# Five of six half gates as fixed-order groups with seven-product pairs, block sums one piece later, and an adding DMA for part of FF2's sums

## The chip, the cores and the metric

The kernel runs on one core of one Trainium2 chip. The metric is the device time of one execution in microseconds (us). Before the change three runs took 1454.71, 1454.83 and 1456.06 us, with a median of 1454.83.

## The reference

The kernel computes one layer of a decoder trunk on 256 tokens of width D = 2048, in float32. The three token mixers (attention, gated linear attention, gated MLP) give y_a, y_b and y_c; they lie ahead of the change. What follows is

```
merged = sigmoid(ga)*(y_a @ wa) + sigmoid(gb)*(y_b @ wb) + sigmoid(gc)*(y_c @ wc)
h   = x + merged @ w_o
out = h + square(relu(rms_norm(h, g2) @ w1)) @ w2      # D_FF = 8192
```

Here ga, gb and gc (2048 columns each) are columns of rms_norm(x, g1) @ w_in; y_a and y_c are 512 wide, y_b is 1024 wide.

## The kernel before, in words

**Float32 by three products.** TensorE multiplies in fp32r. Each operand is split in a high part (a copy to fp32r by ScalarE, "hi") and a rest (a subtraction by VectorE, "lo"), and each product of a 128x128 activation block and a 128x512 weight block is three matmuls: hi*hi, hi*lo, lo*hi. Weights stream from HBM in 1 MB loads and are split on the way, so every weight costs ScalarE and VectorE one pass each.

**Groups of fixed order.** From w_o on, the work is a list of groups. A group makes 256 x 1024 outputs from 2048 rows of weights: eight pairs `kp` of 128-row weight blocks, taken in the order `ORDER`. A pair is a 2x2 by 2x2 block product (two token halves, two row blocks, two column halves). `P` pairs do it with eight block products (24 matmuls, one piece). `S` pairs do it with seven (Winograd's form of Strassen's algorithm: 21 matmuls) in two pieces, `A` (9 matmuls) and `B` (12). An `S` pair needs sums of weight blocks (tile `fsum`, lines 807 to 809) and sums of activation blocks (lines 683 to 689; tiles `hS`, `fS`, `mS`), and four more accumulators, `P1`, `P5`, `P6`, `P7`, beside `c11` to `c22`: all eight PSUM banks. `seven` folds them into a tile `fu` at the group's last piece. w_o has two groups; then come four phases (`ph`), each of two groups of FF1 and two of FF2 (n = 0, 1).

**Order of work.** Inside `manual_schedule` TensorE, ScalarE, VectorE and SyncE run in the order in which the code issues. At piece i the loop issues `ready(i + 2)` (load, weight sums, split), then the matmuls of piece i; there are three buffers for split weights (`fhi`, `flo`) and three for raw ones (`fraw`), so the split of piece i+2 waits until TensorE has finished piece i-1. What a group leaves (turning its result into the next operand by eight TensorE transposes per half, line 664, splitting it, and its block sums) is issued during the first pieces of the next group. The norm of h before FF1 needs only 1/rms per token: its square is multiplied in when FF2's result is added to h (line 914).

**The gates before.** The six half gates (three gates, two column halves; the code takes them in four 512-column steps) and the branch products run in `group_a`, with two-row-block pieces of 12 matmuls, no seven-product pairs, and a sigmoid and a multiplication per 512 columns (lines 691 to 726).

Line 768 is every matmul of the groups, 794 and 795 the split, 221 to 223 the matmuls of `group_a`, 203 and 204 its split.

Of the kernel before, what the change touches and what calls it, by code (L numbers as in the profile page):

```python
# [63 lines left out]
def trunk(ctx: ExitStack, tc: tile.TileContext, x, rpe_table, norm1_g, w_in, q_norm_g, k_norm_g,  # L64
# [626 lines left out]
    mg, mS = None, {}
    for n in range(D // 512):
        gts = []
        for i in range(3):
            pg = group_a(w_in[0], 0, KT, C_GATE + i * D + n * 512, 512, xT)
            if mg is None:
                drain()
                br_ctx.__exit__(None, None, None)
                early_ctx.__exit__(None, None, None)
                mpool = ctx.enter_context(tc.tile_pool(name="mpool", bufs=1))  # L700
                mg_ctx = tc.tile_pool(name="mg", bufs=1)
                mg = mg_ctx.__enter__()
                mT = mpool.tile([P, KT, 2 * T], F32R, tag="act2", name="mT")
            if i == 0 and n == D // 512 - 1:
                gt = [mpool.tile([P, 512], F32, tag="half", name="half", bufs=2) for tt in range(NT)]
            else:
                gt = mg.tile([P, NT, 512], F32, tag=f"gt{i}", name=f"gt{i}", bufs=1 + (i == 0))
                gt = [gt[:, tt, :] for tt in range(NT)]
            for tt in range(NT):
                nc.scalar.activation(gt[tt], pg[tt], AF.Sigmoid, scale=r[:, tt:tt + 1])  # L710
            gts.append(gt)
        for i, (wsrc, k0, nk) in enumerate(((w_br_a, 0, 4), (w_br_b, 4, 8), (w_br_c, 12, 4))):
            pp = group_a(wsrc[0], 0, nk, n * 512, 512, yT, k0=k0)
            for tt in range(NT):
                nc.vector.tensor_mul(gts[i][tt], pp[tt], gts[i][tt])
                if i:
# [283 lines left out]
```

## Time and profile before

| what | number |
|---|---|
| median of three runs | 1454.83 us |
| the profiled execution: own time, span | 1454.36 us, 1452.6 us |
| TensorE, VectorE, ScalarE busy | 1422.9, 1072.9, 766.5 us |
| gates and branches, 296.90 to 649.00 | 352.10 us |
| w_o, 649.00 to 742.68 | 93.68 us |
| first phase of FF, 742.68 to 925.09 | 182.41 us |
| second phase, 925.09 to 1098.92 | 173.83 us |

The stages are cut at the first matmul of each. Phases three and four repeat the second. Matmuls overlap in the trace (one is shown for about 390 ns and the next starts 227 ns later), so waits of TensorE are read from the starts, not from its busy share.

### The profile page before, as it was taken

What the parts mean: (1) busy time and instruction counts of PE and PEld (TensorE: products, weight loads), DVE (VectorE), ACT (ScalarE), POOL (GpSimd) and SP (SyncE); (2) the same over time, 40 slices, a digit from 0 to 9 for tenths busy, and PEclk for the clock granted to TensorE, in tenths of its full rate; (3) what the DMA queues carried; (4) which work ended last, traced back from release to release, by engine and by line L of the source; (5) the groups of instructions that cost most, each with busy time, mean ns of one, the idle gap of its engine ahead of it and who ended that gap; (6) DMA issues with size and microseconds to landing.
All of it is one profiled execution on the core that took longest, in us unless ns stands there. A gap on an engine that the chain in (4) does not pass through costs nothing.

```text
span 1452.6 us, 16287 instructions
## 1 busy us (share of the span) xinstructions
PE 1422.9 (98%) x6452; PEld 1168.5 (80%) x6452; DVE 1072.9 (74%) x1160; ACT 766.5 (53%) x827; POOL 14.0 (1%) x37
## 2 busy tenths in 40 slices
PE   8999999999999999999998999999999999999998
PEld 6899887788888888877886878888788887888776
DVE  5655655454645546457898989999999999999898
ACT  7457444454444444445656654466644665546653
POOL 2000000000000000000000000000000000000000
PEclk9999999999999999999999999999999999999999
DMA  8555554545555555545555555666456555555553
GB/s 290 183 181 165 182 176 133 184 151 199 192 185 203 177 199 187 190 158 193 199 185 192 173 175 197 208 203 203 147 200 207 199 203 174 201 190 194 198 195 124
DMA packets 101948, 272.20 MB, mean 187 GB/s; under 512 B 4748, under 2 KB 11440, under 8 KB 101872
## 3 DMA queue, kind: packets, MB, share of 16 engines
q1 hardware_dynamic: 100944, 268.59, 55.0%
q0 software_dynamic: 928, 2.57, 0.5%
q8 instruction: 50, 0.82, 0.2%
q14 instruction: 26, 0.21, 0.0%
HBM read 268.26 MB, written 2.88 MB: 187 GB/s over the span
## 4 chain that ended last, share of the span: by engine, by line
PE 70%; DVE 18%; issue 6%; ACT 5%; DMA 0%; SPq 0%; DVEq 0%; ACTq 0%
PE c L768 22%; PE ga L221 14%; PE ga L223 14%; PE ga L222 14%; DVE flo L795 8%; PE P L768 4%; DVE fsum L807 3%; ACT fhi L794 3%; DVE fsum L808 2%; DVE fsum L809 2%; PE tt L235 1%; DVE fT L175 1%; PE pst L590 0%; ACT sums L688 0%; ACT half L675 0%
## 5 line engine op out<-in xcount | busy, mean ns | idle before, releaser
L204 DVE TENSOR_TENSOR wlo<-wraw,whi 128x1024 fp32r<-128x1024 f32 (+3 forms) x232 | 266.2, 1152 | 248.6 <-ACT whi L203 248.4
L203 ACT ACTIVATE whi<-wraw 128x1024 fp32r<-128x1024 f32 (+3 forms) x232 | 231.4, 1002 | 292.4 <-PE ga L223 284.9
L794 ACT ACTIVATE fhi<-fraw 128x2048 fp32r<-128x2048 f32 (+2 forms) x145 | 252.9, 1750 | 163.6 <-PE c L768 115.3
L795 DVE TENSOR_TENSOR flo<-fraw,fhi 128x2048 fp32r<-128x2048 f32 (+2 forms) x145 | 300.0, 2080 | 48.0 <-ACT fhi L794 48.0
L221 PE MATMUL ga<-whi,xT 128*128 128x512 f32 (+2 forms) x768 | 297.8, 388 | 0.0
L222 PE MATMUL ga<-wlo,xT 128*128 128x512 f32 (+2 forms) x768 | 293.4, 382 | 0.0
L223 PE MATMUL ga<-whi,xT 128*128 128x512 f32 (+2 forms) x768 | 293.1, 382 | 0.0
L768 PE MATMUL c<-fhi,hT 128*128 128x512 f32 x736 | 237.7, 390 | 0.0
L768 PE MATMUL c<-fhi,fT 128*128 128x512 f32 x736 | 237.1, 390 | 0.0
L221 PEld LDWEIGHTS ga<-whi,xT 128*128 128x128 f32 x768 | 144.6, 188 | 29.8 <-issue 3.9
L223 PEld LDWEIGHTS ga<-whi,xT 128*128 128x128 f32 x768 | 144.6, 188 | 26.9
L222 PEld LDWEIGHTS ga<-wlo,xT 128*128 128x128 f32 x768 | 144.7, 188 | 25.0
L768 PEld LDWEIGHTS c<-fhi,hT 128*128 128x128 f32 x736 | 138.2, 188 | 28.6
L768 PEld LDWEIGHTS c<-fhi,fT 128*128 128x128 f32 x736 | 138.2, 188 | 28.4
L794 ACT ACTIVATE fhi<-fsum 128x1024 fp32r<-128x1024 f32 x104 | 108.6, 1059 | 85.7 <-DVE fsum L807 41.0
L768 PE MATMUL c<-flo,fT 128*128 128x512 f32 x368 | 143.7, 391 | 3.3 <-DVE flo L795 3.3
L768 PE MATMUL c<-flo,hT 128*128 128x512 f32 x368 | 143.2, 389 | 0.0
L795 DVE TENSOR_TENSOR flo<-fsum,fhi 128x1024 fp32r<-128x1024 f32 x104 | 122.5, 1219 | 1.4 <-ACT fhi L794 1.4
L768 PE MATMUL P<-fhi,sums 128*128 128x512 f32 x312 | 106.0, 394 | 4.2 <-ACT fhi L794 4.0
L768 PEld LDWEIGHTS c<-flo,fT 128*128 128x128 f32 x368 | 69.1, 188 | 19.1 <-DVE flo L795 4.9
L768 PEld LDWEIGHTS c<-flo,hT 128*128 128x128 f32 x368 | 69.1, 188 | 14.1
L768 PEld LDWEIGHTS P<-fhi,sums 128*128 128x128 f32 x312 | 59.3, 190 | 18.4 <-ACT fhi L794 6.3
(260 smaller groups left out, 1427.1 us busy)
## 6 DMA issues: line engine op xcount, KB each, us to landing
fraw<-in_w_ff_dram SPq DMA_DIRECT2D x128, 1024.0 KB, 5.0
wraw<-in_w_in_dram SPq DMA_DIRECT2D x80, 1024.0 KB, 4.9
fraw<-in_w_o_dram SPq DMA_DIRECT2D x16, 1024.0 KB, 5.3
wraw<-in_w_br_b_dram SPq DMA_DIRECT2D x8, 1024.0 KB, 5.0
wraw<-in_w_in_dram SPq DMA_DIRECT2D x8, 692.0 KB, 4.1
wraw<-in_w_br_a_dram SPq DMA_DIRECT2D x4, 1024.0 KB, 4.9
wraw<-in_w_br_c_dram SPq DMA_DIRECT2D x4, 1024.0 KB, 5.4
wraw<-in_w_in_dram SPq DMA_DIRECT2D x6, 512.0 KB, 11.4
```

Source lines behind the costliest of these rows:

```text
L175: nc.vector.tensor_tensor(lo, ps, hi.bitcast(F32), ALU.subtract)
L203: nc.scalar.activation(hi[:, j:j + per, :w], src, AF.Copy)
L204: nc.vector.tensor_tensor(lo[:, j:j + per, :w], src, hi[:, j:j + per, :w].bitcast(F32), ALU.subtract)
L221: mm(ps[tt][:, :w], xh, hi[:, j, :w], start=(k == 0), stop=False)
L222: mm(ps[tt][:, :w], xh, lo[:, j, :w], start=False, stop=False)
L223: mm(ps[tt][:, :w], xl, hi[:, j, :w], start=False, stop=(k == nk - 1))
L768: mm(self.banks[role], a, w, start=(n == 0), stop=(n == self.total[role] - 1))
L794: nc.scalar.activation(hi[:, i:e], src[:, i - a:e - a], AF.Copy)
L795: nc.vector.tensor_tensor(lo[:, i:e], src[:, i - a:e - a], hi[:, i:e].bitcast(F32), ALU.subtract)
L807: nc.vector.tensor_tensor(ts[:, 0:2], raw[:, 1:3], raw[:, 0:1].to_broadcast([P, 2, GW]), ALU.add)
L808: nc.vector.tensor_add(ts[:, 2], ts[:, 0], raw[:, 2])
L809: nc.vector.tensor_add(ts[:, 3], ts[:, 2], raw[:, 3])
```

## The change

- Half gate (a, columns 0 to 1023) stays in `group_a` form. While its second 512 columns run, the block sums of x for pairs 2, 3, 5 and 6 are made from fresh transposes of h, which still holds x (`xs_turn`: 16 transposes).
- The other five half gates become groups with `ORDER_G`: pairs 2, 3, 5, 6 with seven products, the rest with eight. The branch products become groups of 2, 4 and 2 `P` pieces; half 0 runs first, then half 1. The merged result is turned into yT's memory.
- w_o keeps two seven-product pairs, now 2 and 3, in the order P0 P1 P6 P7 S2 P4 S3 P5. FF1 and FF2 keep three.
- `weight_sums` for an `A` piece is issued one piece earlier. `block_sums` are issued one piece after the turn, and their split one piece after that. The squares for the norm move one piece later.
- 1/rms is multiplied in at FF1's relu (line 906 of the new kernel); r2 gets its square root and one refining step. In phases 0 to 2 FF2 adds only its four `c` banks to h by VectorE; the tile `fu` is added to h by one accumulating DMA of 1 MB from GpSimd's queue (line 938). `fu` has three buffers; hS takes two of them for the whole FF part.

```diff
-ORDER_O = "P0 P1 P2 P3 P4 S6 S7 P5".split()
+ORDER_O = "P0 P1 P6 P7 S2 P4 S3 P5".split()
+ORDER_G = "P0 P1 S2 S3 P4 S5 S6 P7".split()
...
+    def block_sums(a, s):
+        b = a.rearrange("p j (t c) -> p (j t) c", c=P)
+        nc.vector.tensor_sub(b[:, 3], b[:, 1], b[:, 3])
...
+        def split():
+            nc.scalar.activation(s[:, 0], b, AF.Copy)
+            nc.vector.tensor_tensor(s[:, 1], b, s[:, 0].bitcast(F32), ALU.subtract)
+        return split
...
+    def weight_sums(q, raws):
+        raw = raws[q]
+        ts = ffp.tile([P, 4, GW], F32, tag="fsum", name="fsum")
...
             def relu(c):
                 for tt in range(NT):
-                    nc.scalar.activation(u[:, 2 * tt + c], u[:, 2 * tt + c], AF.Relu)
-            relu(1)
+                    nc.scalar.activation(u[:, 2 * tt + c], u[:, 2 * tt + c], AF.Relu,
+                                         scale=r2[:, tt:tt + 1])
...
-            nc.vector.scalar_tensor_tensor(hv, src, r2[:, tt:tt + 1], hv, op0=ALU.mult, op1=ALU.add)
+            nc.vector.tensor_add(hv, src, hv)
...
         def first(g):
-            u = seven(g)
-            for tt, c in ((0, 1), (1, 1), (0, 0), (1, 0)):
-                into(tt, c, u[:, 2 * tt + c])
+            g.u = u = seven(g)
+            if ends:
+                for tt, c in ((0, 1), (1, 1), (0, 0), (1, 0)):
+                    into(tt, c, u[:, 2 * tt + c])
...
+            if not ends:
+                nc.gpsimd.dma_start(h[:, :, n * W2:(n + 1) * W2], g.u.rearrange("p (t c) w -> p t (c w)", t=NT),
+                                    accum_op=ALU.add)
...
+    def branch_in(i, hf):
+        def last(g):
+            u = gates[i, hf]
+            for tt in range(NT):
+                for c in (1, 0):
+                    v = u[:, 2 * tt + c]
+                    nc.vector.tensor_mul(v, g.banks[f"c{tt + 1}{2 - c}"], v)
+            if i:
+                m = gates[0, hf]
+                nc.vector.tensor_add(m, m, u)
...
+    for hf in range(2):
+        for i, (wsrc, k0, nk) in enumerate(((w_br_a, 0, 4), (w_br_b, 4, 8), (w_br_c, 12, 4))):
+            if (i, hf) != (0, 0):
+                groups.append(Group(w_in[0], 0, C_GATE + i * D + hf * W2, xT, xS, ORDER_G, *gate_in(i, hf)))
+            groups.append(Group(wsrc[0], 0, hf * W2, yT, {}, [f"P{j}" for j in range(nk // 2)], *branch_in(i, hf), k0))
...
+            if i + 1 < len(pieces) and pieces[i + 1][1] == "A":
+                weight_sums(pieces[i + 1][3], raws)
```

**VectorE, first pieces of FF2's first group**, from the weight sums of its first seven-product pair (fsum) on. In the names `flo` is a weight rest, `fT` FF2's activations, `half` the tile in which block sums are made, `sums` and `kinds` where their rest goes. Before:

```order
L807 TENSOR_TENSOR fsum<-fraw 128x1024
L808 TENSOR_TENSOR fsum<-fsum,fraw 128x512
L809 TENSOR_TENSOR fsum<-fsum,fraw 128x512
L795 TENSOR_TENSOR flo<-fraw,fhi 128x1536
L175 TENSOR_TENSOR fT<-half,fT 128x2x256 x2
L683 TENSOR_TENSOR half<-half 128x128
L684 TENSOR_TENSOR half<-half 128x128
L685 TENSOR_TENSOR half<-half 128x128
L686 TENSOR_TENSOR half<-half 128x128
L689 TENSOR_TENSOR sums<-half,sums 128x512
L795 TENSOR_TENSOR flo<-fsum,fhi 128x1024 x2
L795 TENSOR_TENSOR flo<-fraw,fhi 128x2048
```

After:

```order
L781 TENSOR_TENSOR flo<-fraw,fhi 128x1536
L688 TENSOR_TENSOR half<-half 128x128
L689 TENSOR_TENSOR half<-half 128x128
L690 TENSOR_TENSOR half<-half 128x128
L691 TENSOR_TENSOR half<-half 128x128
L180 TENSOR_TENSOR fT<-half,fT 128x2x256 x2
L781 TENSOR_TENSOR flo<-fsum,fhi 128x1024 x2
L688 TENSOR_TENSOR half<-half 128x128
L689 TENSOR_TENSOR half<-half 128x128
L690 TENSOR_TENSOR half<-half 128x128
L691 TENSOR_TENSOR half<-half 128x128
L695 TENSOR_TENSOR kinds<-half,kinds 128x512
```

The weight sums now stand ahead of these rows, the second half of fT ahead of the second block sums, and the rest of the block sums (`kinds`) no longer right behind the sums but a piece later; ScalarE's copies for it move in the same way.

**VectorE, end of an FF2 group**, from `seven` on. Before:

```order
L840 TENSOR_TENSOR fu<-fu,P_6310 128x512
L841 TENSOR_TENSOR fu<-fu,P_6306 128x512
L842 TENSOR_TENSOR fu<-P_6302,fu 128x512
L843 TENSOR_TENSOR fu<-P_6302,fu 128x512
L914 SCALAR_TENSOR_TENSOR h<-fu,r_4800,h 128x512 x4
L795 TENSOR_TENSOR flo<-fraw,fhi 128x2048
L914 SCALAR_TENSOR_TENSOR h<-c_6136,r_4800,h 128x512
L914 SCALAR_TENSOR_TENSOR h<-c_6140,r_4800,h 128x512
L914 SCALAR_TENSOR_TENSOR h<-c_6150,r_4800,h 128x512
L914 SCALAR_TENSOR_TENSOR h<-c_6154,r_4800,h 128x512
L795 TENSOR_TENSOR flo<-fraw,fhi 128x2048
```

After:

```order
L832 TENSOR_TENSOR fu<-fu,P_6335 128x512
L833 TENSOR_TENSOR fu<-fu,P_6331 128x512
L834 TENSOR_TENSOR fu<-P_6327,fu 128x512
L835 TENSOR_TENSOR fu<-P_6327,fu 128x512
L781 TENSOR_TENSOR flo<-fraw,fhi 128x2048
L921 TENSOR_TENSOR h<-c_6165,h 128x512
L921 TENSOR_TENSOR h<-c_6169,h 128x512
L921 TENSOR_TENSOR h<-c_6179,h 128x512
L921 TENSOR_TENSOR h<-c_6183,h 128x512
L781 TENSOR_TENSOR flo<-fraw,fhi 128x2048
```

The four additions of `fu` to h are gone (a DMA of GpSimd's queue does them), and the four of the banks are plain additions.

**VectorE, end of the last branch group, ahead of w_o.** `wlo`, `gt` and `half` are the old form's weight rest and gates, `yT` the merged operand, `c` the branch product, `fu` gates and merged sum. Before:

```order
L715 TENSOR_TENSOR gt_4496<-ga_4679,gt_4496 128x512
L717 TENSOR_TENSOR half<-half,gt_4496 128x512 x2
L715 TENSOR_TENSOR gt_4637<-ga_4752,gt_4637 128x512
L717 TENSOR_TENSOR half<-half,gt_4637 128x512
L715 TENSOR_TENSOR gt_4637<-ga_4753,gt_4637 128x512
L717 TENSOR_TENSOR half<-half,gt_4637 128x512
L795 TENSOR_TENSOR flo<-fraw,fhi 128x1024 x2
L795 TENSOR_TENSOR flo<-fraw,fhi 128x2048 x3
```

After:

```order
L688 TENSOR_TENSOR half<-half 128x128
L689 TENSOR_TENSOR half<-half 128x128
L690 TENSOR_TENSOR half<-half 128x128
L691 TENSOR_TENSOR half<-half 128x128
L977 TENSOR_TENSOR fu<-c_4742,fu 128x512
L977 TENSOR_TENSOR fu<-c_4738,fu 128x512
L977 TENSOR_TENSOR fu<-c_4756,fu 128x512
L977 TENSOR_TENSOR fu<-c_4752,fu 128x512
L980 TENSOR_TENSOR fu<-fu 128x2048
L781 TENSOR_TENSOR flo<-fraw,fhi 128x2048
```

Where multiplications and additions of 512 columns stood, block sums (the second four of eight), four multiplications and a 2048-column addition now stand; w_o's second turn needs that addition.

## Rows read from the trace of the kernel before

**Rows 1.** Page, part 1: engine, busy us (share of span) xinstructions.
```profile
PE 1422.9 (98%) x6452; PEld 1168.5 (80%) x6452; DVE 1072.9 (74%) x1160; ACT 766.5 (53%) x827; POOL 14.0 (1%) x37
```

**Rows 2.** Chain that ended last: start us, us, engine, tile, line, instructions.
```profile
1178.47 11.56 PE c L768 x51
```

**Rows 3.** Windows: stretch us, busy PE PEld DVE ACT POOL, clock, DMA share, GB/s.
```profile
296.90:649.00 352.10, 352.10 (x1571) 291.51 (x1569) 185.57 (x183) 157.79 (x164) 0.00 (x0) 1.00 0.57 188
...
649.00:742.68 93.68, 89.83 (x398) 73.12 (x396) 77.02 (x80) 50.48 (x53) 0.00 (x0) 0.98 0.58 197
...
742.68:925.09 182.41, 175.42 (x781) 142.90 (x780) 165.26 (x173) 107.09 (x109) 0.00 (x0) 0.99 0.55 184
...
925.09:1098.92 173.83, 171.57 (x765) 140.23 (x764) 158.94 (x156) 97.98 (x87) 0.00 (x0) 1.00 0.57 194
...
1010.60:1057.04 46.44, 44.45 (x200) 35.77 (x199) 42.01 (x47) 28.36 (x29) 0.00 (x0) 1.00 0.52 181
...
1057.04:1098.92 41.88, 41.77 (x184) 34.27 (x183) 38.42 (x36) 20.82 (x15) 0.00 (x0) 1.00 0.60 204
...
1140.81:1184.43 43.62, 43.57 (x200) 35.93 (x199) 40.07 (x41) 27.97 (x28) 0.00 (x0) 1.00 0.56 190
...
652.10:655.40 3.30, 3.30 (x9) 2.52 (x9) 2.99 (x2) 0.00 (x0) 0.00 (x0) 0.50 0.94 344
```

**Rows 4.** Timeline, TensorE: start us, us, line, tiles [idle before <- releaser].
```profile
651.81 0.61 PE L768 MATMUL c<-flo,mT 128*128 128x512 f32 x1 [2.42 <-DVE flo L795]
...
762.63 0.39 PE L768 MATMUL c<-fhi,hT 128*128 128x512 f32 x1
...
767.02 0.50 PE L768 MATMUL P<-fhi,sums 128*128 128x512 f32 x1 [4.00 <-ACT fhi L794]
...
1030.95 0.50 PE L768 MATMUL P<-fhi,sums 128*128 128x512 f32 x1
...
1032.21 0.50 PE L768 MATMUL P<-flo,sums 128*128 128x512 f32 x1 [0.76 <-DVE flo L795]
```

**Rows 5.** Timeline, TensorE, eight transposes and the matmul behind them.
```profile
664.22 1.03 PE L235 MATMUL tt<-ident,half 128*128 128x128 f32 x8
...
665.01 0.48 PE L768 MATMUL c<-fhi,mT 128*128 128x512 f32 x1
```

**Rows 6.** Timeline, ScalarE, in the group from 1010.60.
```profile
1029.31 0.63 ACT L688 ACTIVATE sums<-half 128x512 fp32r<-128x512 f32 x1 [3.85 <-DVE half L686]
```

**Rows 7.** Timeline, VectorE, in the same group.
```profile
1033.68 2.29 DVE L795 TENSOR_TENSOR flo<-fraw,fhi 128x2048 fp32r<-128x2048 f32 x1 [0.39 <-ACT fhi L794]
...
1045.13 1.75 DVE L795 TENSOR_TENSOR flo<-fraw,fhi 128x1536 fp32r<-128x1536 f32 x1
```

**Rows 8.** Groups by line and shape: xcount | busy us, mean ns | idle before.
```profile
L795 DVE TENSOR_TENSOR flo<-fraw,fhi 128x2048 fp32r<-128x2048 f32 x91 | 206.7, 2287 | 48.0 <-ACT fhi L794 48.0
...
L795 DVE TENSOR_TENSOR flo<-fsum,fhi 128x1024 fp32r<-128x1024 f32 x104 | 122.5, 1219 | 1.4 <-ACT fhi L794 1.4
...
L795 DVE TENSOR_TENSOR flo<-fraw,fhi 128x1536 fp32r<-128x1536 f32 x52 | 91.1, 1751 | 0.0
...
L807 DVE TENSOR_TENSOR fsum<-fraw 128x1024 f32<-128x1024 f32 x52 | 63.5, 1222 | 0.6
...
L685 DVE TENSOR_TENSOR half<-half 128x128 f32<-128x128 f32 x17 | 5.0, 293 | 0.6
...
L841 DVE TENSOR_TENSOR fu<-fu,P 128x512 f32<-128x512 f32 x18 | 12.4, 687 | 0.6
...
L914 DVE SCALAR_TENSOR_TENSOR h<-fu,r,h 128x512 f32<-128x512 f32 x32 | 21.9, 747 | 0.0
```

**Rows 9.** DMA issues: count, KB each, median us from issue to landing.
```profile
fraw<-in_w_ff_dram SPq DMA_DIRECT2D x128, 1024.0 KB, 5.0
...
bdram<-brow POOLq DMA_DIRECT2D x2, 384.0 KB, 2.6
...
bias<-bdram POOLq DMA_DIRECT2D x1, 512.0 KB, 7.2
```

More of the change, by code (lines that the diff above doesn't have):

```diff
@@ L691, in trunk @@
[L691 to L716, printed above, removed]
-                    nc.vector.tensor_add(gts[0][tt], gts[0][tt], gts[i][tt])
-        later()
-        ks = [n * 4, n * 4 + 2]
-        srcs = [[gts[0][tt][:, (2 * jp + j) * P:(2 * jp + j + 1) * P] for j in range(2) for tt in range(NT)]
-                for jp in range(2)]
-        if n < D // 512 - 1:
-            for k, s in zip(ks, srcs):
-                later(lambda k=k, s=s: turn_into(mT, [k], [s]))
-        else:
-            later(lambda: turn_into(mT, ks, srcs, None, mS))
@@ L739, in trunk, with __init__ @@
-    r2 = gpool.tile([P, NT], F32, name="r2")
-    hs = gpool.tile([P, NT], F32, name="hs")
+                rest.append(lambda a=a, s=kinds[k // 2]: block_sums(a, s))
+        return both(rest)
     W2 = 2 * GW
     class Group:
-        def __init__(self, src, r0, c0, act, sums, order, first, last):
+        def __init__(self, src, r0, c0, act, sums, order, first, last, k0=0):
             self.src, self.r0, self.c0, self.act, self.sums, self.order = src, r0, c0, act, sums, order
+            self.k0 = k0
@@ L933, in trunk @@
+    for n in range(2):
+        groups.append(Group(w_o[0], 0, n * W2, mT, mS, ORDER_O, *residual(n)))
     for ph in range(FF // D):
[L934 removed]
         for n in range(2):
[L936 removed]
+            groups.append(Group(w_ff1[0], 0, ph * D + n * W2, "hT", hS, ORDER, *square_in(ph, n)))
         for n in range(2):
[L938 removed]
+            groups.append(Group(w_ff2[0], ph * D, n * W2, "fT", fS, ORDER, *add_in(ph, n)))
@@ L965, in trunk @@
             ready(i + LEAD)
-            since = i - done
-            if since == 1 and after:
-                after[0]()
-            multiply(piece, wts.pop(i), half=after[2] if since == 2 and after else None)
-            if since == 1 and after:
-                after[1]()
-            if since == 2 and len(after) > 3:
-                after[3]()
-            step()
+            run(i, "early")
+            multiply(piece, wts.pop(i), half=lambda: run(i, "half"))
+            run(i, "half")
+            run(i, "late")
             if ends:
-                after, done = g.last(g), i
+                for (d, when), fn in zip(((1, "early"), (1, "late"), (2, "half"), (3, "early")), g.last(g)):
+                    todo.setdefault((i + d, when), []).append(fn)
 _INS = ['x', 'rpe_table', 'norm1_g', 'w_in', 'q_norm_g', 'k_norm_g', 'gla_lr_w', 'gla_lr_b', 'gla_out_g',
```

186 lines of the change are left out of this document (133 added, 53 removed).

## The prediction

> **What bounds the kernel now.** I read the page first: TensorE is busy 98% of the span, VectorE 74%, ScalarE 53% [rows 1]. A busy TensorE may still be waiting, so the next thing is its pace. In the chain that ended last, 51 matmuls of 128x512 take 11.56 us where nothing stops them, 0.2267 us each [rows 2]. Eight transposes take 0.79 us from the first to the next matmul, 0.099 each [rows 5]. With these two prices each stage of the windows [rows 3] is checked: what is left is time in which TensorE stood still.
>
> Gates and branches: 1536 matmuls are 348.2 us, the other 35 instructions about 3.5, together 351.7 of 352.10. No waits. VectorE is busy only 185.57 us there. A phase of FF: 4 groups of 5 x 24 + 3 x 21 = 183 matmuls are 165.9 us, 32 transposes 3.2, together 169.1 of 173.83: 4.7 us of waits. By groups: a group without turns needs 41.5 us and with 16 transposes 43.1. The first FF2 group takes 46.44 (3.4 lost), the second 41.88 (0.4), FF1's first the same, FF1's second 43.62 (0.55). The first phase takes 182.41, 8.6 more than the second; 1.6 of that are 16 transposes for hT, 7.0 are waits in FF1's first group. w_o: 372 matmuls (84.3), 24 transposes (2.4), so 7.0 of 93.68 are lost.
>
> The timeline shows who is waited for. In FF2's first group the seven-product piece B of pair 3 gets its split late: TensorE starts at 1030.95 and next at 1032.21, waiting for VectorE's `flo` [rows 4], and ScalarE had stood 3.85 us at its copy of block sums which VectorE was still making [rows 6]. Everything queued behind that copy, the splits included, came late. In FF1's very first group it is the same, with four squares behind it: TensorE stands from 762.63 to 767.02 for ScalarE's `fhi`. w_o begins with 2.42 us for VectorE [rows 4]; in the stretch from 652.10 the granted clock is 0.50, the 1.2 GHz level, with 9 matmuls in 3.30 us, which costs 3.30 - 9 x 0.2267 = 1.3 us [rows 3].
>
> The 0.4 us of the quiet groups come from another place. Pairs 5 and 6 follow each other. A seven-product pair asks of VectorE 1.22 + 2 x 0.69 for the sums, 1.75 and 2 x 1.22 for the splits, 6.8 us [rows 8], against 21 x 0.2267 = 4.76 us of TensorE. VectorE can't start this earlier, since P4's split waits for a buffer of TensorE (0.39 idle), and 11.45 us pass from that split to the split of A6 [rows 7].
>
> **The change, part by part.** *Matmuls.* Each half gate with four seven-product pairs has 4 x 24 + 4 x 21 = 180 matmuls for 192. Five of them save 60 x 0.2267 = 13.6 us. The 16 transposes for x's block sums cost 1.6. All of it lies on TensorE's stream: **-12.0**.
>
> *VectorE in the gates.* A half gate now asks 4 x 6.8 + 4 x 2.29 + 8 x 0.69 = 41.8 us of VectorE [rows 8] against 180 x 0.2267 = 40.8 of TensorE. The branch groups behind it give some back: for b (four pieces, four multiplications, one 2048-column addition at a split's 2.29) 14.2 against 21.8, for c 9.6 against 10.9, for a 7.3 against 10.9. Over the five gates and six branches VectorE has 271, with two turns 278, of 291 us. So the cover is thin, but it holds on the whole; S5 and S6 stand where they stand in FF, so each gate should lose what a quiet FF group loses, 0.39. Five times that is **+2.0**. Both ends: 0 (VectorE has run ahead), and 2 us for each of the five gates' last two pairs, with nothing saved up, 5 x 2 x (6.8 - 4.76) = 20.
>
> *Into w_o.* From the end of the last gate VectorE's queue holds a split 2.29, four additions 2.75, a split 2.29, two rests 1.37, a split 2.29, eight block sums of 0.29, four multiplications 2.75 and the addition 2.29: 18.4 us [rows 8]. TensorE asks for that sum after two branch pieces, eight transposes and one w_o piece, 10.9 + 0.8 + 5.4 = 17.1. That is 1.3 us of waiting if VectorE never stands, and up to 5 with a stand like that of rows 6. I take 4, plus 1.3 for a fallen clock and 0.7 for the rest, 6 in place of 7: **-1.0**, between -4 and +2.
>
> *FF1's first group.* The block sums' copies leave ScalarE's way and the squares come one piece later. VectorE's queue up to P4: splits 2.29, 2.29, 1.75 and 2.44, four additions 2.75, weight sums 2.6, four rests 2.75, eight block sums 2.3, one more rest 0.69, 19.9 us, against 16.3 + 1.6 of TensorE up to A3's start; the split of P4 waits for ScalarE's squares. From there 11.45 to A6's split, with another rest 0.69 and about 1 us (an estimate: seven tiny instructions) for the root. A6's split would end near 35, TensorE asks at 33. With about 1 us at P4 and A5 I get 3.0 for 7.0: **-4.0**, between -6.5 and 0.
>
> *FF2's first group, four times.* The same sum, without squares and root: P4's split can begin at 19.9, A6's at 19.9 + 11.45 + 0.69 = 32.0, and it ends at 33.7; TensorE asks at 33.1. So 0.6, taken as 1.0, for 3.4. The other three groups keep theirs: order and buffers round P4, S5, S6 are as before, and weight sums issued a piece earlier stand at the same place of VectorE's queue there. 4 x 2.4: **-10**, between -14 and 0.
>
> *The adding DMA.* It takes four additions of 0.747 us from VectorE in six groups, and four more get 0.06 shorter [rows 8], 19 us of VectorE in all. They stood at the end of a group, ahead of P pieces, where VectorE has slack. I cost it at **nothing**; if that slack is gone, a part of the -10 hangs on it. New waits: the DMA waits for the four bank additions, and nothing else is queued on GpSimd. The next `seven` waits for the DMA, since hS holds two of the three `fu` buffers: ScalarE's first copy of `seven`, with the splits of the next group queued behind it, and TensorE behind those. From issue to that copy there are 41.5 - 5.4 - 4.7 = 31 us (a group, less its last piece, less the split and additions ahead of the issue). The nearest rows: 1 MB of weights lands in 5.0 us; GpSimd's queue took 2.6 for 384 KB and 7.2 for 512 KB [rows 9]. At the slowest of these, and twice over because h is read too, 1 MB takes 28.8. It fits. I take 10.
>
> The Trainium skill, page SBUF - State Buffer, section Who interferes with whom, says that VectorE with two SBUF inputs excludes a GpSimd instruction that reads SBUF, and that a DMA "stalled" by VectorE is one whose descriptors GpSimd could not write. No run here shows an adding DMA beside such work; it would lengthen the 10 us and is in the third rival below.
>
> Sum: -12.0 + 2.0 - 1.0 - 4.0 - 10 = -25. The profiled execution took 1454.36 us (a span of 1452.6 and 1.8 round it), 0.5 below the median of the runs. 1454.4 - 25 = **1429**.
>
> **Rivals.** *VectorE becomes the bound of the gates.* For it: 41.8 against 40.8, and only two pieces of lead. Against it: quiet FF groups ask 31.8 + 5.5 = 37.3 of VectorE and lose only 0.4 with the same sequence at their end. It costs 12 to 20 us in place of 2: about 1443. Chance 0.17.
>
> *FF keeps its waits.* For it: VectorE's queue in FF2's first group is as long as before but for 3 us. Against it: ScalarE's stand of 3.85 us, which the new order removes. It takes back up to 14: about 1441. Chance 0.13.
>
> *VectorE is what limits FF everywhere.* For it: 158.94 of 173.83 us, 91% [rows 3]; then its 19 us less come off whole, 9 more than my 10: about 1420. Against it: the 0.39 idle of rows 7. Chance 0.08. The Trainium skill, Perfetto Trace Analysis, section Identifying the Most-Contended Engine, says just this: judge TensorE by its weight loads (here 140.23 of 173.83, 81%) and VectorE by occupancy, so VectorE comes first. The waits counted from starts, 4.7 of 173.83, don't agree with it.
>
> *The adding DMA holds up `seven`: slower.* Six times X - 31 us, X being the time from issue to landing. From X = 35 on it eats the 25 us; at X = 40 the kernel takes about 1483. For it: an adding DMA is in no row. Against it: 28.8 as the slow bound. Chance 0.05.
>
> **Numbers.** My forecast has 0.55, the rivals 0.17, 0.13, 0.08 and 0.05; 0.02 is left for no change. The range from 1419 to 1445 takes in both ends of the middle cases and leaves out the DMA's and the worst gates. A measurement of this kernel tells 0.2%, 2.9 us, from no change. Faster: 0.92, all but the last two. Same: 0.03. Slower: 0.05.
>
> **What would show it.** Gates and branches (to w_o's first matmul) 11 us shorter, with waits of about 0.4 us at the second seven-product pair before each gate's end and nowhere else; ScalarE no longer standing for `half` in FF2's first group, and that group at 44 us; the other groups still 41.9 and 43.6; FF1's first group 4 us shorter; one wait of some 4 us after w_o's first piece; no wait on the software DMA queue. I am wrong if a gate group takes over 43 us, if FF2's first group stays above 46, or if `seven` waits for the DMA.

## The result, and the profile after

The changed kernel takes 1432.64 us (median of four runs, 1430.41 to 1432.99), the kernel before 1454.77 beside it: a ratio of 0.984, with a 95% interval from 0.983 to 0.986. The forecast was 1429, in a range from 1419 to 1445. The profiled execution took 1432.36 us, 22.0 less than that of before.

The page after, engines, queue and issues of the adding DMA (the last number is us from issue to landing), against [rows 1, 9]:

```profile
PE 1408.1 (98%) x6408; PEld 1158.8 (81%) x6408; DVE 1155.1 (81%) x1232; ACT 795.2 (56%) x826; POOL 21.2 (1%) x43
...
q0 software_dynamic: 2560, 8.86, 3.3%
...
h<-fu POOLq DMA_DIRECT2D x6, 1024.0 KB, 9.4
```

The windows after, by stage and then by group, in the columns of [rows 3]: gates and branches, w_o, the first and the second phase, w_o's first group, FF1's first group, FF2's two groups of phase 2.

```profile
297.90:643.52 345.62, 342.61 (x1517) 281.57 (x1516) 290.25 (x272) 185.84 (x156) 0.00 (x0) 1.00 0.58 198
643.52:733.77 90.25, 88.15 (x406) 73.05 (x404) 76.73 (x82) 51.36 (x57) 0.00 (x0) 1.00 0.54 181
733.77:909.56 175.79, 173.13 (x782) 141.89 (x781) 161.33 (x172) 107.72 (x111) 1.24 (x1) 1.00 0.60 198
909.56:1081.19 171.63, 170.72 (x766) 140.39 (x764) 152.30 (x148) 97.77 (x87) 2.40 (x2) 1.00 0.65 209
643.52:689.80 46.28, 44.18 (x204) 36.49 (x203) 38.79 (x43) 24.29 (x23) 0.00 (x0) 1.00 0.51 169
733.77:779.82 46.05, 44.21 (x201) 35.77 (x200) 44.64 (x56) 30.77 (x39) 0.00 (x0) 1.00 0.54 182
995.05:1039.31 44.26, 43.60 (x201) 35.92 (x199) 41.41 (x46) 28.21 (x29) 0.00 (x0) 1.00 0.57 191
1039.31:1081.19 41.88, 41.77 (x185) 34.27 (x183) 35.57 (x32) 20.82 (x15) 1.19 (x1) 1.00 0.73 229
```

Stage by stage against [rows 3]: gates and branches 352.10 to 345.62 (-6.5), w_o 93.68 to 90.25 (-3.4), the first phase 182.41 to 175.79 (-6.6), each later phase 173.83 to 171.6 (-2.2). Ahead of the gates the time is 1.0 us longer (the stretch begins at 297.90, not at 296.90). A gate group takes 41.20 us (42.11 where eight transposes lie in it); VectorE's work in gates and branches has grown from 185.57 to 290.25.

Two timelines tell what is new. ScalarE after, where the second 512 columns of the first half gate begin:

```profile
312.67 1.06 ACT L208 ACTIVATE whi<-wraw 128x1024 fp32r<-128x1024 f32 x1 [1.47 <-issue]
319.42 0.69 ACT L1046 ACTIVATE fu<-ga,r 128x512 f32<-128x512 f32 x1 [5.69 <-PE ga L228]
320.78 0.69 ACT L1046 ACTIVATE fu<-ga,r 128x512 f32<-128x512 f32 x1 [0.67 <-PE ga L228]
321.37 2.94 ACT L208 ACTIVATE whi<-wraw 128x1024 fp32r<-128x1024 f32 x3
```

TensorE after: at the same place, into w_o, and in FF2's first group:

```profile
320.36 0.39 PE L228 MATMUL ga<-whi,xT 128*128 128x512 f32 x1
322.47 0.51 PE L226 MATMUL ga<-whi,xT 128*128 128x512 f32 x1 [1.72 <-ACT whi L208]
323.73 0.80 PE L227 MATMUL ga<-wlo,xT 128*128 128x512 f32 x1 [0.75 <-DVE wlo L209]
...
648.74 0.39 PE L754 MATMUL c<-fhi,yT 128*128 128x512 f32 x1
651.22 0.98 PE L240 MATMUL tt<-ident,fu 128*128 128x128 f32 x7 [2.10 <-DVE fu L980]
...
1028.12 0.39 PE L754 MATMUL P<-fhi,fT 128*128 128x512 f32 x1
1029.16 0.50 PE L754 MATMUL P<-flo,fT 128*128 128x512 f32 x1 [0.66 <-DVE flo L781]
```

The sigmoid of the first 512 columns is issued ahead of the weight splits of the next 512, and it needs the end of the matmuls. ScalarE stands 5.69 us, then splits three weights in a row, and TensorE waits twice, 1.88 + 1.03 us from start to start (less one pitch). No step of the forecast had this place.

### The profile page after: what moved, and what is told of

Read it like the earlier page. It is cut to its first block, busy times and chain, and to the rows that moved or that the text cites. A ratio compares the mean times of both kernels' runs of the same rounds, so it can differ in the third digit from the quotient of the medians.

```text
span 1430.7 us, 16240 instructions
## 1 busy us (share of the span) xinstructions
PE 1408.1 (98%) x6408; PEld 1158.8 (81%) x6408; DVE 1155.1 (81%) x1232; ACT 795.2 (56%) x826; POOL 21.2 (1%) x43
## 4 chain that ended last, share of the span: by engine, by line
PE 72%; DVE 18%; issue 5%; ACT 4%; DMA 0%; SPq 0%; DVEq 0%; ACTq 0%
PE c L754 41%; DVE flo L781 9%; PE ga L226 7%; PE ga L227 7%; PE ga L228 7%; PE P L754 6%; DVE fsum L787 4%; ACT fhi L780 3%; DVE fsum L788 2%; DVE fsum L789 2%; PE tt L240 1%; PE pst L595 0%; PE po L619 0%; DMA h<-in_x_dram 0%; PE po L614 0%
## 5 line engine op out<-in xcount | busy, mean ns | idle before, releaser
L780 ACT ACTIVATE fhi<-fraw 128x2048 fp32r<-128x2048 f32 (+2 forms) x201 | 352.9, 1757 | 292.0 <-PE c L754 231.4
L781 DVE TENSOR_TENSOR flo<-fraw,fhi 128x2048 fp32r<-128x2048 f32 (+2 forms) x201 | 416.7, 2083 | 92.8 <-ACT fhi L780 90.7
L209 DVE TENSOR_TENSOR wlo<-wraw,whi 128x1024 fp32r<-128x1024 f32 (+3 forms) x120 | 128.7, 1082 | 101.6 <-ACT whi L208 101.4
L208 ACT ACTIVATE whi<-wraw 128x1024 fp32r<-128x1024 f32 (+3 forms) x120 | 112.4, 946 | 120.4 <-PE ga L228 113.3
L226 PE MATMUL ga<-whi,xT 128*128 128x512 f32 (+2 forms) x448 | 174.2, 390 | 1.7 <-ACT whi L208 1.7
L227 PE MATMUL ga<-wlo,xT 128*128 128x512 f32 (+2 forms) x448 | 170.1, 380 | 0.8 <-DVE wlo L209 0.8
L228 PE MATMUL ga<-whi,xT 128*128 128x512 f32 (+2 forms) x448 | 169.6, 379 | 0.0
L754 PE MATMUL c<-fhi,yT 128*128 128x512 f32 x464 | 146.4, 390 | 0.0
L754 PE MATMUL P<-fhi,kinds 128*128 128x512 f32 x432 | 144.7, 389 | 0.0
L754 PE MATMUL c<-fhi,xT 128*128 128x512 f32 x400 | 130.7, 389 | 0.0
L226 PEld LDWEIGHTS ga<-whi,xT 128*128 128x128 f32 x448 | 85.1, 190 | 19.7 <-issue 3.9
L228 PEld LDWEIGHTS ga<-whi,xT 128*128 128x128 f32 x448 | 85.1, 190 | 14.6
```

The lines of the kernel that those rows point to most:

```text
L208: nc.scalar.activation(hi[:, j:j + per, :w], src, AF.Copy)
L209: nc.vector.tensor_tensor(lo[:, j:j + per, :w], src, hi[:, j:j + per, :w].bitcast(F32), ALU.subtract)
L226: mm(ps[tt][:, :w], xh, hi[:, j, :w], start=(k == 0), stop=False)
L227: mm(ps[tt][:, :w], xh, lo[:, j, :w], start=False, stop=False)
L228: mm(ps[tt][:, :w], xl, hi[:, j, :w], start=False, stop=(k == nk - 1))
L754: mm(self.banks[role], a, w, start=(n == 0), stop=(n == self.total[role] - 1))
```

## The experiments

Every kernel but the last two is the changed kernel with the edit shown; each was timed beside the kernel before. Single executions of the changed kernel lie 2.6 us apart, but a group's length repeats to 0.05 us where TensorE's clock does not fall, so small effects are read from group lengths. Below, "w_o", "FF1" and "FF2" are w_o's first group (46.3 us), FF1's first group of phase 1 (46.1) and FF2's first groups (44.2).

| kernel | median us | ratio to before (95%) | w_o | FF1 | FF2 |
|---|---|---|---|---|---|
| changed | 1432.64 | 0.984 (0.983 to 0.986) | 46.3 | 46.1 | 44.2 |
| sums in the turn | 1444.48 | 0.993 (0.992 to 0.994) | 51.3 | 51.1 | 45.0 |
| VectorE adds | 1430.84 | 0.983 (0.982 to 0.985) | 46.3 | 46.1 | 44.2 |
| weight sums late | 1431.37 | 0.984 (0.983 to 0.985) | 47.9 | 45.3 | 44.2 |
| relu early | 1433.31 | 0.985 (0.984 to 0.986) | 47.9 | 46.1 | 44.2 |
| sums and relu | 1451.62 | 0.998 (0.997 to 0.999) | 50.9 | 52.3 | 46.6 |
| all order undone | 1449.25 | 0.996 (0.995 to 0.997) | 51.2 | 50.1 | 46.4 |
| split with the sums | 1454.20 | 0.999 (0.999 to 1.000) | 50.9 | 52.3 | 45.6 |
| sigmoid behind | 1427.86 | 0.981 (0.980 to 0.983) | 46.3 | 46.1 | 44.2 |
| one seven-product pair | 1439.75 | 0.989 (0.988 to 0.991) | 46.3 | 46.1 | 44.3 |
| three moves | 1423.29 | 0.978 (0.977 to 0.980) | 44.1 | 44.3 | 44.3 |
| pairs apart | 1422.25 | 0.977 (0.976 to 0.979) | 44.1 | 44.2 | 44.2 |
| four pairs in FF | 1498.74 | 1.030 (1.029 to 1.031) | 46.9 | 53.6 | 51.2 |

**Block sums back in the turn.**

```diff
-                rest.append(lambda a=a, s=kinds[k // 2]: block_sums(a, s))
+                if dst is not None:
+                    block_sums(a, kinds[k // 2])()
+                else:
+                    rest.append(lambda a=a, s=kinds[k // 2]: block_sums(a, s))
```

> The changed kernel (1432.6 us), but the block sums of a turn and their copy and rest are issued inside the turn again (hT, fT, mT; x's stay deferred). Theory: ScalarE's copy of block sums, waiting for VectorE at the head of ScalarE's queue, was what cost FF2's first groups and FF1's first group their time, so both come back: FF2's first groups from 44.2 to about 46.4 us, four times 2.2, and the first phase's FF1 first group about 3 us longer; together +10 to +13, 1443 to 1446 us. Rival (the shorter VectorE queue, through the adding DMA and the additions taken from it, is what shortened these groups): they stay near 44.2 to 45, and the time within 1432 to 1436 us.

+11.8 us, the size expected, but the place is not: w_o lost 5.1, FF1 5.0, FF2's first groups only 0.8 each and not 2.2. So the deferral is worth most where the forecast had least, and something else carries 1.4 of the 2.2 in FF2.

**No adding DMA.**

```diff
-            if ends:
-                for tt, c in ((0, 1), (1, 1), (0, 0), (1, 0)):
-                    into(tt, c, u[:, 2 * tt + c])
+            for tt, c in ((0, 1), (1, 1), (0, 0), (1, 0)):
+                into(tt, c, u[:, 2 * tt + c])
...
-            if not ends:
-                nc.gpsimd.dma_start(h[:, :, n * W2:(n + 1) * W2], g.u.rearrange("p (t c) w -> p t (c w)", t=NT),
-                                    accum_op=ALU.add)
```

> The changed kernel (1432.6 us), but no adding DMA: in all FF2 groups VectorE adds the four sums to h at the group's end, as before. Theory: VectorE has slack at that place, and the DMA was worth nothing: 0 to +1.5 us, 1432 to 1434 us, with FF2's first groups at 44.2 and the FF1 groups behind an FF2 group at 41.9. Rival (VectorE limits FF everywhere, so its additions count whole): six times 4 x 0.747 and four times 0.06 a group, about +18 us, 1450 us. Middle (a part of the 2.2 us in FF2's first groups hung on VectorE's slack): +2 to +9.

Nothing, as expected: 1.8 us less in the median, inside the spread. FF2's second group in this kernel's windows, with four additions more on VectorE (37.94 us for 35.57) and the length unchanged:

```profile
1039.54:1081.42 41.88, 41.77 (x185) 34.27 (x183) 37.94 (x36) 20.84 (x15) 0.00 (x0) 1.00 0.60 204
```

**Weight sums late.**

```diff
-            if i + 1 < len(pieces) and pieces[i + 1][1] == "A":
-                weight_sums(pieces[i + 1][3], raws)
...
-            split2(hi, lo, 0, 3, raw[0][:, 1:4])
+            weight_sums(q, raws)
+            split2(hi, lo, 0, 3, raw[:, 1:4])
```

> The changed kernel (1432.6 us), but the sums of a seven-product pair's weights are made when its piece A is prepared, as before, and not behind the piece that goes ahead of it. Theory: the order on VectorE's queue barely changes, so 0 to +1.5 us, 1432 to 1434. Rival (the sums a step earlier are what lets the splits of the seven-product pieces come in time): TensorE waits again ahead of the pieces of type B, some 1 us in each of 13 groups with turns, 1440 to 1446 us.

Nothing in FF (44.2; FF1 even 0.8 shorter). The 1.6 us in w_o is TensorE's clock, which fell behind the same wait of 2.26 us, told at the end.

**Relu early, and what goes with it.** Three kernels: relu alone; with the block sums; with the weight sums too.

```diff
+            relu(1)
...
-            return [lambda: (relu(1), relu(0)) and None, lambda: turns(made["fT"], n, 1, src, None, fS, AF.Square),
+            return [lambda: relu(0), lambda: turns(made["fT"], n, 1, src, None, fS, AF.Square),
```

> The changed kernel (1432.6 us), but relu(1) of an FF1 group is issued at that group's end, as before, ahead of the next weight split on ScalarE's queue (relu(0) stays behind it). Undoing the deferred block sums gave back 0.8 of the 2.2 us in each first FF2 group, so something else carries the rest. Theory now: the first relu waits at the head of ScalarE's queue for VectorE's sums, the split of P1 behind it comes late, and VectorE stands for that split; so each first FF2 group goes from 44.2 to 45 to 45.6 us, +3 to +6 in four phases. Rival (each of the two waits is hidden as long as the other is gone): 44.2 to 44.5 and at most +1 us.

> The changed kernel (1432.6 us) with the block sums inside the turn and relu(1) at the FF1 group's end, but the weight sums a step ahead as in the changed kernel. Block sums alone cost 0.8 us in each first FF2 group, relu alone nothing, weight sums alone nothing, the three together 2.2. Theory: the relu is the partner that brings the other 1.4 (a split of weights late on ScalarE, VectorE standing for it): 46.4 us in the first FF2 groups, about 1450 us. Rival (the weight sums are the partner): 45.05 us, about 1444.5 us as with the block sums alone.

> The changed kernel (1432.6 us) with all three moves of order undone at once: block sums inside the turn, relu(1) at the group's end, weight sums in the preparation of piece A. Theory: in the FF groups this is the order of the kernel before, so FF2's first groups are back at 46.4 us and with w_o and the first FF1 group (5 us each, as with the block sums alone) the time is +18 to +20, 1451 us. Rival (the adding DMA, or where the buffers now lie, carries part of it): first FF2 groups stay at 45 to 45.5, 1444 to 1447 us.

The rival holds for relu alone: 44.26 us, nothing. Together with the block sums it brings the group to 46.59, and with the weight sums as well to 46.42, as in [rows 3] (46.44). The FF2 group of phase 2, in the windows of the kernel with block sums alone:

```profile
1005.06:1050.10 45.04, 43.89 (x201) 35.84 (x200) 41.80 (x46) 28.24 (x29) 0.00 (x0) 1.00 0.54 186
```

with block sums and relu:

```profile
1006.55:1053.14 46.59, 44.44 (x200) 35.77 (x199) 41.93 (x46) 28.09 (x29) 0.00 (x0) 1.00 0.54 180
```

and with all order undone:

```profile
1004.22:1050.64 46.42, 44.48 (x200) 35.77 (x199) 41.96 (x46) 28.08 (x29) 0.00 (x0) 1.00 0.53 183
```

VectorE's work is the same in all (41.8 to 42.0). Zero and 0.8 apart, 2.4 together: two holds on the same stretch of ScalarE's queue. What counts is when ScalarE comes to the split of pair 4. Its rows for relu alone (the stand at relu, then this split), for the block sums alone, for both, and for the kernel before, each in FF2's first group of phase 2:

```profile
1000.58 1.34 ACT L906 ACTIVATE fu<-fu,r 128x512 f32<-128x512 f32 x2 [5.07 <-DVE fu L902]
...
1016.91 1.92 ACT L780 ACTIVATE fhi<-fraw 128x2048 fp32r<-128x2048 f32 x1 [2.91 <-PE c L754]
...
1024.81 3.27 ACT L783 ACTIVATE fhi<-fraw 128x2048 fp32r<-128x2048 f32 x2
...
1027.84 3.28 ACT L783 ACTIVATE fhi<-fraw 128x2048 fp32r<-128x2048 f32 x2
...
1031.75 3.27 ACT L794 ACTIVATE fhi<-fraw 128x2048 fp32r<-128x2048 f32 x2
```

Counted from the group's first matmul (998.61, 1005.06, 1006.55 and 1010.60), the split starts at 18.3 us with relu alone, as in the changed kernel, and ScalarE waits 2.91 us for TensorE ahead of it: the 5.07 us at relu have been made up. With the block sums it starts at 19.75, with both at 21.3, before at 21.15, each time without a pause, and the group ends 25.3 us after it (45.04, 46.59, 46.45). A hold costs what is left of it at that split.

**The split right behind the sums.** This keeps the delay of a piece and puts only ScalarE's wait back.

```diff
-        def split():
-            nc.scalar.activation(s[:, 0], b, AF.Copy)
-            nc.vector.tensor_tensor(s[:, 1], b, s[:, 0].bitcast(F32), ALU.subtract)
-        return split
+        nc.scalar.activation(s[:, 0], b, AF.Copy)
+        nc.vector.tensor_tensor(s[:, 1], b, s[:, 0].bitcast(F32), ALU.subtract)
```

> The changed kernel (1432.6 us), with the block sums put off by one piece as in it, but their copy on ScalarE and their rest on VectorE issued right behind them and not one piece later again. With everything inside the turn, w_o's first group and FF1's first group lost 5 us each and FF2's first groups 0.8 each. Theory A: the loss is ScalarE's stand at the copy, behind which the weight splits queue; the stand is there again, so most of it comes back: 51, 50 and 45 us for these groups, 1442 to 1444 us. Theory B: the loss is VectorE's order, the sums standing ahead of a turn's or a weight's rests within the same piece; one piece of delay is enough, so the groups stay at 46.3, 46.1 and 44.2, 1432 to 1435 us.

Theory A, and more of it than was expected: 50.9, 52.3 and 45.6 us, and 1454.2 in all, as much as the whole change gains. These groups give 16.5 of the 20.6 us by which the profiled execution (1452.98 us) is longer. The edit reaches further than they do: the copies for x's block sums stand right behind their sums too, TensorE waits 3.9 us between 339 and 349 us, and the first branch group starts 2.8 us later; w_o's second group takes 1.25 more. ScalarE in FF1's first group of this kernel:

```profile
757.46 0.63 ACT L693 ACTIVATE kinds<-half 128x512 fp32r<-128x512 f32 x1 [4.95 <-DVE half L691]
...
765.15 0.63 ACT L693 ACTIVATE kinds<-half 128x512 fp32r<-128x512 f32 x1 [2.67 <-DVE half L691]
```

and TensorE behind it:

```profile
770.08 0.80 PE L752 MATMUL c<-fhi,hT 128*128 128x512 f32 x1 [4.44 <-ACT fhi L778]
```

ScalarE stands twice for VectorE's sums, the squares and the split of pair 4 queue behind, and TensorE waits 4.6 us (start to start less a pitch) for that split. The same two copies, one piece later, wait for nothing. ScalarE in FF2's first group after the change, the answer to [rows 6]:

```profile
1009.83 0.61 ACT L694 ACTIVATE kinds<-half 128x512 fp32r<-128x512 f32 x1
1013.36 1.92 ACT L780 ACTIVATE fhi<-fraw 128x2048 fp32r<-128x2048 f32 x1 [2.91 <-PE c L754]
1015.18 0.61 ACT L694 ACTIVATE kinds<-half 128x512 fp32r<-128x512 f32 x1
```

The idle time there now ends with TensorE, which frees a buffer: ScalarE has caught up.

**One seven-product pair in a gate.**

```diff
-ORDER_G = "P0 P1 S2 S3 P4 S5 S6 P7".split()
+ORDER_G = "P0 P1 P2 P3 P4 S5 P6 P7".split()
```

> The changed kernel (1432.6 us), but a half gate has one pair with seven products in place of four (order P0 P1 P2 P3 P4 S5 P6 P7). Theory: TensorE's stream decides in the gates: 5 x 3 x 3 matmuls of 0.2267 us come back, +10.2; 12 transposes of 0.099 fewer, -1.2; and since no two seven-product pairs follow each other, the waits of 0.38 in each gate go, -1.9: +7.1 us, about 1439.7, a gate group at 189 x 0.2267 = 42.85 us without a wait. Rival (VectorE is the bound of the gates): fewer sums and splits, so the gates get no longer, and the time is the same or less, 1428 to 1433 us.

1439.75 against 1439.7 expected. A gate group in its windows; the 189 matmuls run without a wait while VectorE has 27.25 us to do:

```profile
358.86:401.70 42.84, 42.84 (x190) 35.48 (x189) 27.25 (x21) 17.42 (x11) 0.00 (x0) 1.00 0.57 196
```

With less work on VectorE the gates got longer, by the matmuls: TensorE is their bound.

**The sigmoid behind the splits.**

```diff
-        first_sigmoid(0)
         ps = [bank(f"ga{tt}") for tt in range(NT)]
...
         ahead.append(next(src))
         ahead.append(next(src))
+        first_sigmoid(0)
```

> The changed kernel (1432.6 us), but the first sigmoid of gate (a) is issued behind the first two weight splits of its second 512 columns and not ahead of them. Theory: the sigmoid, which waits for the end of the group before it, holds up the splits on ScalarE's queue, and TensorE so loses 1.88 + 1.03 + 0.36 us to waits and about 1.4 us to the clock that fell to 0.50; with the splits first all of that goes: -4.5 us, 1428 us, no wait of TensorE over 0.3 us between 318 and 328 us and no stretch there at 0.50. Rival (the splits wait for something else, a buffer or the weights' DMA): the wait stays, 1432 to 1433 us.

As expected: -4.8 in the median, and the first branch group starts 4.5 us earlier (344.14 for 348.68). TensorE's row in its windows has no gap:

```profile
319.00:325.00 6.00, 6.00 (x30) 4.94 (x30) 2.43 (x2) 3.56 (x6) 0.00 (x0) 1.00 0.62 207
```

**Three moves.** The sigmoid as above; the branch product by column halves; the squares of w_o's second half seven pieces later.

```diff
-            for tt in range(NT):
-                for c in (1, 0):
+            for c in (1, 0):
+                for tt in range(NT):
                     v = u[:, 2 * tt + c]
                     nc.vector.tensor_mul(v, g.banks[f"c{tt + 1}{2 - c}"], v)
+                    if i:
+                        w = gates[0, hf][:, 2 * tt + c]
+                        nc.vector.tensor_add(w, w, v)
...
+            if n:
+                todo.setdefault((at[0] + 10, "late"), []).append(norm)
-                    lambda: turns(made["hT"], n, 0, src, n2c, hS, AF.Copy), norm]
+                    lambda: turns(made["hT"], n, 0, src, n2c, hS, AF.Copy), None if n else norm]
```

> The changed kernel (1432.6 us) with three moves: the first sigmoid of gate (a) behind the two weight splits (alone 1427.9); the multiplications and the last addition of a branch made by column halves, the half that the next turn wants first; the squares of w_o's second half and the root two thirds of a group later. Theory: -4.6 for the first; TensorE's wait of 2.26 us in w_o's first group goes, -2.2; the waits of 0.45 and 1.71 us in FF1's first group go in part, -1.5 to -2; together 1424 us. Rivals: the wait in w_o comes from the rests and block sums ahead of the branch sums, then w_o's first group stays at 46.3; the wait at A6 in FF1's first group comes from VectorE's queue and not from the squares, then that group stays at 46.

1423.29: faster than the changed kernel by 9.4 us. w_o's first group came down to its matmuls and transposes, without a wait, and FF1's to one late split (0.8 us), in its windows:

```profile
639.42:683.52 44.10, 44.10 (x204) 36.53 (x202) 39.23 (x46) 24.40 (x23) 0.00 (x0) 1.00 0.53 176
727.49:771.74 44.25, 43.59 (x200) 35.94 (x199) 43.54 (x51) 30.22 (x38) 0.00 (x0) 1.00 0.56 188
```

**Pairs apart, and four pairs in FF.** Both on the kernel with three moves; in the first, ORDER_Q is taken by the FF groups without turns. The second is made with the split right behind the sums.

```diff
+ORDER_Q = "P0 P1 P2 S3 S6 P4 S5 P7".split()
-ORDER_G = "P0 P1 S2 S3 P4 S5 S6 P7".split()
+ORDER_G = "P0 S2 S3 P1 S5 P4 S6 P7".split()
```

> The kernel with three moves (1423.3 us), and the seven-product pairs put apart where no turns lie in the group: gates P0 S2 S3 P1 S5 P4 S6 P7, the second FF2 group and FF1's first from the second phase on P0 P1 P2 S3 S6 P4 S5 P7. Theory: the 0.38 us a group come from two seven-product pairs in a row behind a single P piece, so they go in 5 gates and 7 FF groups: 12 x 0.38 = -4.5, about 1418.8 us. Rival (VectorE is then late at the pairs near the group's begin, where the sums of the group before and the branch's multiplications lie): the waits move there and grow, 1423 to 1432 us.

Half right. The seven FF groups lose their wait, the gates do not: two of five run without one (40.80), three wait longer. Gate (a) of half 1 and FF2's second group in its windows:

```profile
471.09:512.92 41.83, 41.10 (x181) 33.71 (x180) 38.67 (x36) 22.82 (x17) 0.00 (x0) 1.00 0.57 189
1031.88:1073.36 41.48, 41.48 (x185) 34.35 (x183) 35.81 (x32) 20.71 (x15) 1.19 (x1) 1.00 0.72 230
```

The gates gave back 0.7, FF gained 2.8, and the median moved 1.0.

```diff
-ORDER = "P0 P1 P2 S3 P4 S5 S6 P7".split()
+ORDER = "P0 P1 S2 S3 P4 S5 S6 P7".split()
```

> The kernel with three moves (1423.3 us), but four seven-product pairs in every FF group too (order P0 P1 S2 S3 P4 S5 S6 P7), and the copy and rest of the block sums right behind the sums. TensorE's stream alone would give 16 x 3 x 0.2267 = -10.9 us, 1412 us. Theory: here VectorE becomes the bound, which it was not in the gates: a pair more asks 4.5 us of it; without turns 35.6 + 4.5 = 40.1 of 41.2 us, which just holds, but the two groups with turns go to 46 us of VectorE's work against 42.9 of TensorE's, so 3 to 4 us of waits in each of them: +3 to +5 us a phase, 1435 to 1445 us. Rival (the lead saved up in the quiet groups carries the others): 1412 to 1420 us.

Slower by far more than expected. In its windows FF1's second and FF2's second group of phase 2:

```profile
977.15:1027.47 50.32, 45.28 (x197) 36.16 (x196) 46.09 (x51) 29.78 (x31) 0.00 (x0) 0.97 0.49 166
1078.68:1119.88 41.20, 41.09 (x181) 33.71 (x180) 39.84 (x37) 22.41 (x17) 1.19 (x1) 1.00 0.75 235
```

The quiet group holds at 41.20, as worked out. The group with turns takes 50.3, and VectorE's 46.09 don't fill it: ScalarE stands there again, as its timeline shows.

```profile
993.57 0.63 ACT L693 ACTIVATE kinds<-half 128x512 fp32r<-128x512 f32 x1 [5.37 <-DVE half L691]
```

Since both edits are in this kernel, it doesn't tell how much is VectorE's load alone; that stays open.

## Why the prediction was right, and where it was not

| term | forecast | measured |
|---|---|---|
| matmul stream and gates' own waits | -10 | -10.6 |
| entry into the fixed order | not in the sum | +4.3 |
| gates and branches in all | -10 | -6.5 |
| into w_o | -1.0 | -3.4 |
| FF1's first group | -4.0 | -4.4 |
| FF2's first group, four times | -10 | -8.8 |
| ahead of the gates | 0 | +1.0 |
| sum | -25 | -22.1 |

That the sum came within 3 us is in part luck: of the 4.3 us that were in no term, 2.4 are made up by w_o, which gave more than was forecast.

**Matmul stream and gates: right, but for eight transposes.** The 60 matmuls fewer are 13.6 us. Each gate group takes 41.20 us, 180 x 0.2267 and 0.39; the five and the last branch lose 2.2. TensorE's timelines show 32 transposes in this stage before and 40 after, so 0.8 us more and not 1.6: x's 16 are new, but eight of the merged result have moved into w_o (24 there before, 32 after). The one-pair kernel shows that the stream is the price: its gates get longer by their matmuls and lose their wait. That wait lies at pair 6, behind pair 5; pairs 2 and 3, which follow each other too, have none. VectorE's 41.8 against 40.8 did not decide.

**The step that was missing.** "All of it lies on TensorE's stream" left out the place at which the old loop hands over to the fixed order. The 4.3 us are the waits counted from starts at 320.36 to 326.5: 1.88 + 1.03 + 0.36 and five matmuls 0.20 late each. The kernel with the sigmoid behind the splits gets them back. The diff showed the sigmoid ahead of the splits; what was not asked is when each instruction at the head of an in-order queue becomes ready. Of the gates' -6.5 the two terms make -6.3. The 1.0 ahead is not shown to belong to the change: in the traces of the changed kernel and its variants, whose code is the same up to there, the gates' first matmul starts anywhere between 297.15 (all order undone) and 298.82 us (pairs apart), and before at 297.0.

**Into w_o: mis-sized.** The wait is where the forecast put it, after w_o's first piece, for VectorE's 2048-column addition; it is 2.26 and not 4, and in this execution no clock fell behind it, for which 1.3 had been added. VectorE does stand on the way there, but for less than the 3.85 us of [rows 6], 1.78 for a copy of ScalarE and 1.03 for a split:

```profile
639.46 1.29 DVE L180 TENSOR_TENSOR yT<-half,yT 128x512 fp32r<-128x512 f32 x2 [1.78 <-ACT yT L179]
641.79 2.29 DVE L781 TENSOR_TENSOR flo<-fraw,fhi 128x2048 fp32r<-128x2048 f32 x1 [1.03 <-ACT fhi L780]
```

All of w_o's waits came down from 7.0 to 2.7 us; the eight transposes take 0.8 of it back.

**FF1's first group: right**, 2.6 us of waits for 3.0, at the pieces named: 0.6 at pair 4, 0.3 at A5 and 1.8 at A6.

**FF2's first group: the number right, the reason in part.** The forecast gave the 2.4 us to the copies of block sums, and looked at VectorE's queue up to pair 4. The runs give 0.8 to the copies alone and the rest to the pair of copies and relu, through the start of pair 4's split (18.3 us after the group's first matmul for 21.15 before); relu's move from ahead of a split to behind it stood in the diff and in no term. And VectorE's queue up to pair 4 was no limit: it stands before that split, in the timeline after:

```profile
1015.30 2.29 DVE L781 TENSOR_TENSOR flo<-fraw,fhi 128x2048 fp32r<-128x2048 f32 x1 [2.15 <-ACT fhi L780]
...
1020.10 0.68 DVE L695 TENSOR_TENSOR kinds<-half,kinds 128x512 fp32r<-128x512 f32 x1
...
1027.36 1.75 DVE L781 TENSOR_TENSOR flo<-fraw,fhi 128x1536 fp32r<-128x1536 f32 x1
```

From pair 4's split to A6's 12.06 us pass, for 12.14 forecast (11.45 of [rows 7] and a rest of 0.69). That one rest fits what this group waits beyond the quiet ones (1.1 against 0.4): the group ends 25.95 us after ScalarE's split of pair 4, and 25.3 in the kernels where the rest stands ahead of it. Moving it by itself was not tried. The 0.39 us of [rows 7] are not, as the forecast read them, a wait for a buffer of TensorE in the quiet groups: the row lies in FF2's first group, and ScalarE, which it names, went from one split straight into the next.

**The adding DMA: right.** From issue to landing it took a median of 9.4 us for the 10 taken, no instruction waited for it, and it is worth nothing. The Trainium skill, SBUF — State Buffer, section Who interferes with whom, has VectorE with two SBUF inputs exclude only a GpSimd instruction that reads SBUF, and says that in its probe a `tensor_copy` stalled such DMAs and a `tensor_tensor` did not. The forecast joined two of its rules (and the rival that it meant is the fourth). Here the DMA landed beside a VectorE busy for 35.57 of 41.88 us; whether the 9.4 us hold a delay no run shows.

**The rivals.** VectorE as bound of the gates falls by the one-pair kernel. FF keeping its waits is what happens if the deferral and relu's move are undone together. VectorE as the limit of FF falls by the kernel without the DMA: 2.4 us more of VectorE in a group, the same 41.88. The Trainium skill's rule in Perfetto Trace Analysis, section Identifying the Most-Contended Engine, judges TensorE by MFU (the share of its peak that the matmuls reach) and by the busy share of its weight loads. By the weight loads, which alone the forecast took, VectorE (35.57 of 41.88, 85%) would come before TensorE (82%); the measurement decides against that here. What the largest waits have in common is another thing: an instruction at the head of ScalarE's or VectorE's queue waits for another engine, and work that is ready stands behind it. The Trainium skill, PSUM — Partial Sum Buffer, section Engine vs sequencer instructions, states in passing that these queues are strict first in, first out. The traces agree, with stands of ScalarE of 5.69 us at a sigmoid and 4.95 at a copy.

## What to carry to other kernels

When an engine runs in the order of the code, go through its queue at each place that the change touches and ask of each instruction when its operand is ready; a small one (0.6 us) that waits for another engine costs what the work queued behind it is late: compare the start of that work, counted from the group's begin, with the time at which it is needed. Put an instruction that waits behind the work that is ready, by one piece for each engine that its operand passes: sums, then copy, then rest. Undo moves singly and in pairs, since two holds that cost nothing and 0.8 us apart cost 2.4 together; and test what looks like the clever part (here the DMA) by itself.

## What the runs showed of the hardware

TensorE's clock does not follow from the program alone. Behind the same two waits at 320 us, 1.88 and 1.03 in each of nine traces, the mean granted clock of the next 5.5 us was 0.69 in the changed kernel, at 0.50 in a stretch within:

```profile
322.47:328.00 5.53, 4.78 (x15) 3.63 (x16) 3.47 (x3) 1.84 (x2) 0.00 (x0) 0.69 0.37 104
...
323.20:326.60 3.40, 2.88 (x7) 2.32 (x8) 2.74 (x3) 1.11 (x2) 0.00 (x0) 0.50 0.20 23
```

1.00 in the kernel with the block sums in the turn:

```profile
322.75:328.30 5.55, 4.79 (x22) 3.73 (x23) 3.48 (x3) 2.85 (x5) 0.00 (x0) 1.00 0.36 103
```

and 0.56 in the kernel with relu early. In the same time TensorE started 15, 22 and 11 matmuls.

```profile
322.80:328.30 5.50, 4.74 (x11) 3.55 (x12) 3.48 (x3) 1.84 (x2) 0.00 (x0) 0.56 0.35 110
```

So behind the same waits and the same code the fall to the 1.2 GHz level held up no matmul in four of the nine traces, five in three and ten in two, which costs up to 2 us at 0.20 each. The four without a fall are those of the kernels that undo something of the block sums; whether that is chance, these runs don't tell. Likewise w_o's first group took 47.9 us instead of 46.3 in two kernels (weight sums late, relu early), with eight matmuls late by 0.20 behind the same wait of 2.26. One program differs too: the four runs with relu early took 1430.51 us at a mean granted clock of 1.000, 1433.23 and 1433.38 at 0.998, and 1435.91 at 0.996. How far single runs lie apart does not follow from these two waits: 0.9 us with the pairs apart and 1.5 with the three moves, which have neither, 2.6 in the changed kernel, but 0.8 in the one-pair kernel, which has both.
